# Half-row score matmuls, earlier gate chunks and later low parts in a two-block transformer kernel

## The chip, the cores and the metric

The kernel runs on one core of one Trainium2 chip. The metric is the device time of one execution in microseconds (us), the median of several. Five engines work side by side, each through its own list of instructions in a fixed order: TensorE (PE in the profile, with its weight loads as PEld), VectorE (DVE), ScalarE (ACT), GpSimd (POOL) and SyncE (SP), which only issues DMAs. They wait for each other by semaphores alone.

## The reference, cut to what matters

A token block of 256 rows and 1024 features passes through two layers of a first block and one layer of a second block. All data are float32.

```python
for l in range(2):                                   # first block
    xn = rms_norm(h, norm_g[l])
    a_q, a_k, a_v, i_q, i_k, i_w, ..., c_q, c_k, c_v, ... = split(xn @ w_in[l])
    # dsa: indexer scores of 4 heads, top-64 keys per query, then 8 heads of 64 features, one shared key
    score = einsum('bqh,bqhk->bqk', wi, relu(einsum('bqhd,bkd->bqhk', qi, ki)))
    # diff: 8 heads of 64 features, softmaxes mixed in pairs: p[0] - lam * p[1]
    # (three more branches: mla, sgu, memory)
    h = h + merged_branches @ w_out[l]
x = rms_norm(h, final_norm_g)
# second block
shift_a, scale_a, gate_a, shift_m, scale_m, gate_m = split(silu(c) @ w_ada + b_ada)   # 12 chunks of 512
h = rmsnorm(x, g_mix) * (1 + scale_a) + shift_a
gq, gk, gv, gr, gg, mq, mk, mv = split(h @ w_in)     # gla: 4 heads; moba: 8 heads of 64 features
o_moba = softmax(mq @ mk.T * 64**-0.5 + rel_bias, causal) @ mv
x = x + gate_a * (concat([o_gla, o_moba]) @ w_out)
h = rmsnorm(x, g_mlp) * (1 + scale_m) + shift_m
x = x + gate_m * (relu(h @ w_ff1) ** 2 @ w_ff2)
out = rmsnorm(x, g_final)
```

## The kernel before

**Tiling.** The 256 tokens are two tiles t=0, 1 of 128 rows; features are halves c=0, 1 of 512. Every large product is a sum of three matmuls in the fast float32 form: each operand is split into a high and a low part (`hi`, `lo` of the tokens; `wh` by ACT in L408 and `wl` by DVE in L409 for the weights), and wh·hi, wl·hi, wh·lo are added in PSUM (L470, L471, L473, and L493, L495, L496 for transposed results). A weight piece is 4 x 128 rows by up to 512 columns (1 MB), loaded by SP in the order of a list `pieces`; the loads run ahead as far as buffers are free. A result bank is evacuated by ACT or DVE.

**Order.** While one piece is multiplied, `half(k)` after each of its halves steps three lanes of side work (attention, small norms, the modulation) by one `yield`, and `defer(f, n)` runs f after n halves. A scheduler then orders the instructions of each engine by priority; `pin` keeps chosen instructions in program order, `behind(mark)` holds instructions behind a marked one, `tc.high_priority` pulls a chain ahead. Within an engine the resulting order is fixed.

**Scores.** A head has 64 features, and two heads lie above each other in a tile of 128 partitions. The kernel before multiplies on all 128 rows: `padded` writes the queries of a head into its own 64 rows of a zeroed tile (`qz`, `dz`), so that the other head's keys meet zeros (L973, L1005, L1051, L1474; plain float32, two passes for each matmul); for tile t=1 of dsa, `stacked` puts the high part of the query above its low part, and two fast matmuls (L678, L679) make a score. `attention` runs units of 2 or 4 heads through three stages: `s1` (scores into one PSUM bank, then `soft`: L718 row maximum on DVE, L721 exponent on ACT), `s2` (transposes L748, evacuated by ACT in L751 and DVE in L752) and `s3` (L768, probabilities times values).

**Modulation.** The vector silu(c) @ w_ada is made chunk by chunk by `ada(q, gate)`: two raw pieces of 1 MB, one DVE multiply (L1403) and seven multiply-adds (L1405) over 128x512, a split (L1414, L1415), and two matmuls against ones (L1419, L1420). Chunks 0 to 3 run in layer 0 and 6 to 9 in layer 1 of the first block (table `ADA`); 4 and 5 (`gate_a`) run in the second block while its `w_in` is multiplied, and 10, 11 later.

**Handovers.** At the end of the first block each half row of the residual gets its final norm and the second block's first norm at once (`row_norms`: L1247 adds the branch result, ACT's L694 sums squares, L1328 multiplies by the gain in place, L694 sums again; L1350, L1352 and a reciprocal root by DVE's L247 to L253 follow). `modulated` scales the row (L1358 on DVE and L1359 on ACT) and `to_operand_mod` transposes it on PE (L612), writes the high part on ACT (L654) and the low part by L659, L661 and L662. The same happens after the second block's `w_out` (`residual`, L1703 and L1704). Here PE needs the operand before it can go on.

Of the kernel before, what the change touches and what calls it, by code (L numbers as in the profile page):

```python
# [27 lines left out]
LOOK, AHEAD, WK, SLOTS = 3, 6, 7, 13  # L28
# [6 lines left out]
ADA = [(0, 1, 2, 3), (6, 7, 8, 9)]  # L35
# [22 lines left out]
def block_kernel(ctx: ExitStack, tc: tile.TileContext, a, out):  # L58
# [30 lines left out]
    def work(shape, tag="wk", dt=F32, bufs=None):  # L89
        n = 1  # L90
        for s in shape[1:]:
            n *= s
        own = tag in ("gains0", "gains1", "mb0", "mb1", "q0", "gg")
# [55 lines left out]
    marks = {}  # L149
# [225 lines left out]
    def run_stream():  # L375
# [20 lines left out]
        def split(i, by_k=False):  # L396
# [250 lines left out]
    def to_operand_mod(src, t, xo, am, bm, k0):  # L647

        tmp = work([128, 4, 128])
# [3 lines left out]
        for i, (sc, bi) in enumerate(cols):  # L653
            A.activation(hi[:, i, :], ps[i // 2][:, i % 2, :], AF.Identity, scale=sc, bias=bi)  # L654
        for b in range(0, 4, 2):
            for i in range(b, b + 2):
                sc, bi = cols[i]
                if b == 0 or k0 == 0:
                    V.tensor_scalar(tmp[:, i, :], ps[b // 2][:, i - b, :], sc, bi, op0=OP.mult, op1=OP.add)  # L659
                else:  # L660
                    A.activation(tmp[:, i, :], ps[1][:, i - 2, :], AF.Identity, scale=sc, bias=bi)  # L661
            ins = V.tensor_tensor(lo[:, b:b + 2, :], tmp[:, b:b + 2, :], hi[:, b:b + 2, :].bitcast(F32), OP.subtract)  # L662
        if k0 == 0:
            marks["lo", t] = ins

    def stacked(dst, ps):


        n = ps.shape[1]
        for b in range(2):  # L670
            own, other = (slice(64 * c, 64 * c + 64) for c in (b, 1 - b))
            to = slice(n * b, n * b + n)
            A.activation(dst[own, to, :], ps[own], AF.Copy)
            V.tensor_tensor(dst[other, to, :], ps[own], dst[own, to, :].bitcast(F32), OP.subtract)

    def stacked_mm(ps, q, hi, lo):

        T.matmul(ps, q, hi, start=True, stop=False)  # L678
        T.matmul(ps, q, lo, start=False, stop=True)  # L679

    def padded(dst, ps, scale=1.0):


        n = ps.shape[1]
        for b in range(2):
            own = slice(64 * b, 64 * b + 64)
            A.activation(dst[own, n * b:n * b + n, :], ps[own], AF.Copy, scale=scale)
# [9 lines left out]
    def attention(units, finish, nheads, dv, d=1):  # L697
# [8 lines left out]
        def soft(u, heads):  # L706

            nh, nk = len(heads), u["nk"]
            ps = bbank([128, nh, nk])
            for k, h in enumerate(heads):  # L710
                u["score"](ps[:, k, :], h, u["t"], nk)
# [20 lines left out]
        def s1(i):  # L732
            u = units[i]
            p, rs = soft(u, u["heads"])
            if u.get("combine"):
                p2, rs2 = soft(u, u["heads2"])
# [105 lines left out]
    def layer(l, h):  # L842
# [81 lines left out]
        def dsa_prep():  # L924
# [11 lines left out]
            q0 = work([128, 2, 128], "q0", bufs=1)  # L936

            q1, i1, ks = (slot(d).bitcast(F32R) for d in ([128, 8, 128], [128, 4, 128], [128, 4, 256]))
            yield
            for t in range(2):  # L940
                ps = transpose4(aq[:, t, :])
                if t:
                    stacked(q1, ps)
                else:
                    padded(dz[:, 0:8, :], ps)
                ps = bbank([128, 4, 128])
                for i, src in enumerate((kd[:, t, 0:128], kd[:, t, 128:256], a2[:, t, 128:256],
                                         a2[:, t, 256:384])):
# [14 lines left out]
            for t in range(2):  # L963
                nk = 128 * (t + 1)
                acc = work([128, nk], "acc")
                R = {}
                for b in range(2):
                    ps = bbank([128, 2, nk])
                    for p in range(2):
                        if t:  # L970
                            stacked_mm(ps[:, p, :], i1[:, 2 * b + p, :], ks[:, 1, :], ks[:, 3, :])
                        else:
                            T.matmul(ps[:, p, :], dz[:, 8 + 2 * b + p, :], q0[:, 1, :], start=True, stop=True)  # L973
                    R[b] = work([128, 2, nk], "P")
                    A.activation(R[b], ps, AF.Relu)
# [16 lines left out]
            L["dsa"] = (q0, q1, ks, mb)  # L992
            lanes[0].add(dsa_attn())

        def dsa_attn():
            q0, q1, ks, mb = L["dsa"]
# [3 lines left out]
            def score(ps, hh, t, nk):  # L1000
                i = 4 * (hh % 2) + hh // 2
                if t:
                    stacked_mm(ps, q1[:, i, :], ks[:, 0, :], ks[:, 2, :])
                else:
                    T.matmul(ps, dz[:, i, :], q0[:, 0, :], start=True, stop=True)  # L1005
            units = [dict(t=t, heads=hs, outs=hs, nk=128 * (t + 1), score=score, scale=64 ** -0.5,
                          bias=lambda k, t=t: mb[t], v=lambda hh, b: a2[:, b, 64:128])
# [11 lines left out]
        def diff_prep():  # L1019
# [16 lines left out]
            kT = slot([128, 4, 256])  # L1036
            for t in range(2):
                padded(qz[:, :, tsl(t)], transpose4(cq[:, t, :]))
# [3 lines left out]
            L["diff"] = (kT, nl, dg)  # L1042
            lanes[0].add(diff_attn())

        def diff_attn():
            kT, nl, dg = L["diff"]
# [3 lines left out]
            def score(ps, hh, t, nk):  # L1050
                T.matmul(ps, qz[:, 4 * (hh % 2) + hh // 2, tsl(t)], kT[:, hh // 2, 0:nk], start=True, stop=True)  # L1051
# [272 lines left out]
    def row_norms(t, c):  # L1324
# [3 lines left out]
        V.tensor_tensor(hc, hc, B["fg"][:, c * 512:(c + 1) * 512], OP.mult)  # L1328
# [4 lines left out]
        v = mean_so_far(("y", t), hc, c, 0.0)  # L1333
        if c == 0:
            return
        def back():
# [4 lines left out]
        for c in range(2):  # L1341
            defer(lambda c=c: rest(c), 3 - t)
# [13 lines left out]
    def modulated(t, r, xo, am, bm):  # L1356
# [35 lines left out]
    def ada(q, gate=None):  # L1392

        st = {}
        for j in range(2):
# [13 lines left out]
            def fin():  # L1409
# [11 lines left out]
                if gate is None:  # L1421
# [45 lines left out]
    def moba_attn():  # L1467
        for _ in range(2):
            yield
        kT = B["mT"]  # L1470
        o = slot([128, 2, 512])

        def score(ps, hh, t, nk):
            T.matmul(ps, qz[:, 4 * (hh % 2) + hh // 2, tsl(t)], kT[:, hh // 2, 0:nk], start=True, stop=True)  # L1474
        units = []
        for p in range(2):
            for q in range(2):
# [425 lines left out]
```

## Time and profile before

| | us |
|---|---|
| median of 3 runs (lowest, highest) | 1221.54 (1221.0, 1221.8) |
| the profiled execution | 1220.62 |
| its span, first to last instruction | 1218.9 |
| PE busy | 1201.0 (99%) |
| DVE busy | 904.1 (74%) |
| ACT busy | 672.5 (55%) |
| POOL busy | 34.0 (3%) |

The profile is of one execution. Times are from the span's start. "Busy" is the union of an engine's instructions; matmuls overlap, so the records of one group can sum to more than they cost. Between 30 and 890 us the two layers of the first block run, from 890 to 905 the handover to the second block, from 905 its `w_in`, moba and gla, from 1008 its `w_out`, from 1023 to 1042 the second handover, then the feed-forward part.

### The profile page before, as it was taken

Reading aid. Unit: us, or ns where it says so; the run is one execution under the profiler, and the core shown is the slowest. Engines: PE = TensorE matmul, PEld = TensorE weight load, DVE = VectorE, ACT = ScalarE, POOL = GpSimd, SP = SyncE. Lnnn points to the kernel's source line nnn. Section 1 sums busy time; section 2 is a strip of 40 time slices with the busy share of each in tenths; the row PEclk is TensorE's granted clock in tenths of the full one; section 3 lists DMA queues with packets and bytes.
Section 4 is the critical chain, followed back from the end, with each engine's and each line's share of the span. In section 5 each row is a group of like instructions: output and inputs, shape, how many; then the busy total and the mean of one; then the engine's idle time right before and its main releaser. Section 6 shows DMA issues by size and latency. Waiting matters only on the chain.

```text
span 1218.9 us, 17443 instructions
## 1 busy us (share of the span) xinstructions
PE 1201.0 (99%) x6589; PEld 1039.3 (85%) x6589; DVE 904.1 (74%) x1889; ACT 672.5 (55%) x1188; POOL 34.0 (3%) x68
## 2 busy tenths in 40 slices
PE   9999999999999999999999999999999899999997
PEld 7888988898888888898888988888879787898996
DVE  5996777659886776776877688776788778766755
ACT  5765455547566455546544766654465556545442
POOL 4000000000000000000000000000020010000000
PEclk9999999999999999999999999999999999999999
DMA  9866646454566466655566445655547634666740
GB/s 310 305 230 212 202 141 216 134 175 157 179 210 205 138 219 196 233 174 173 164 221 194 149 151 171 227 190 182 166 138 265 207 114 137 233 218 221 255 145 35
DMA packets 117828, 231.31 MB, mean 190 GB/s; under 512 B 4604, under 2 KB 14496, under 8 KB 117616
## 3 DMA queue, kind: packets, MB, share of 16 engines
q1 hardware_dynamic: 114640, 221.62, 54.6%
q0 software_dynamic: 2640, 7.78, 2.1%
q8 instruction: 52, 0.85, 0.3%
q10 hardware_dynamic: 464, 0.79, 0.2%
q14 instruction: 32, 0.26, 0.1%
HBM read 229.10 MB, written 2.63 MB: 190 GB/s over the span
## 4 chain that ended last, share of the span: by engine, by line
PE 92%; DVE 3%; ACT 2%; DMA 1%; issue 1%; ACTq 0%
PE pm L471 22%; PE pm L470 22%; PE pm L473 22%; PE pm L493 4%; PE pm L495 4%; PE pm L496 4%; PE po L768 3%; PE pm L612 3%; PE pm L748 2%; DMA wt<-in_w_in_dram 1%; PE pm L1164 1%; PE pm L1051 1%; DVE wl L409 1%; ACT j L694 1%; ACT hi L654 1%
## 5 line engine op out<-in xcount | busy, mean ns | idle before, releaser
L409 DVE TENSOR_TENSOR wl<-wt,wh 128x1024 fp32r<-128x1024 f32 (+6 forms) x388 | 443.3, 1170 | 163.6 <-ACT wh L408 162.6
L408 ACT ACTIVATE wh<-wt 128x1024 fp32r<-128x1024 f32 (+6 forms) x388 | 379.6, 1014 | 254.4 <-PE pm L473 141.7
L470 PE MATMUL pm<-wh,hi 128*128 128x512 f32 (+4 forms) x1288 | 500.1, 390 | 0.0
L471 PE MATMUL pm<-wl,hi 128*128 128x512 f32 (+4 forms) x1288 | 490.2, 382 | 0.8 <-DVE wl L409 0.8
L473 PE MATMUL pm<-wh,lo 128*128 128x512 f32 (+4 forms) x1288 | 337.2, 382 | 0.5 <-DVE lo L662 0.5
L471 PEld LDWEIGHTS pm<-wl,hi 128*128 128x128 f32 x1288 | 242.3, 188 | 44.9 <-DVE wl L409 2.1
L470 PEld LDWEIGHTS pm<-wh,hi 128*128 128x128 f32 x1288 | 242.1, 188 | 43.3 <-issue 0.3
L473 PEld LDWEIGHTS pm<-wh,lo 128*128 128x128 f32 x1288 | 237.5, 188 | 47.4 <-DVE lo L662 2.2
L493 PE MATMUL pm<-hi,wh 128*128 128x256 f32 x416 | 118.9, 286 | 0.0
L496 PE MATMUL pm<-hi,wl 128*128 128x256 f32 x416 | 117.7, 283 | 0.0
L495 PE MATMUL pm<-lo,wh 128*128 128x256 f32 x416 | 117.7, 283 | 0.0
L493 PEld LDWEIGHTS pm<-hi,wh 128*128 128x128 f32 x416 | 79.7, 192 | 1.4 <-issue 1.0
L495 PEld LDWEIGHTS pm<-lo,wh 128*128 128x128 f32 x416 | 79.8, 192 | 0.4
L496 PEld LDWEIGHTS pm<-hi,wl 128*128 128x128 f32 x416 | 79.7, 192 | 0.0
L721 ACT ACTIVATE w<-w,s 128x256 f32<-128x256 f32 (+1 forms) x112 | 49.8, 446 | 35.6 <-DVE s L718 35.6
L1405 DVE SCALAR_TENSOR_TENSOR w<-wt,cact,w 128x512 f32<-128x512 f32 x84 | 62.7, 747 | 1.6 <-DMA wt<-in_w_ada_dram 0.6
L768 PEld LDWEIGHTS po<-t,w 128*128 128x128 f32 x352 | 45.9, 191 | 7.0 <-ACT w L751 3.4
L1210 ACT ACTIVATE t<-pm,s 128x512 f32<-128x512 f32 x40 | 27.5, 689 | 40.7 <-PE pm L473 40.6
L768 PE MATMUL po<-t,w 128*128 128x64 f32 (+1 forms) x352 | 45.2, 270 | 3.3 <-ACT w L751 3.0
L612 PE MATMUL pm<-ident,t 128*128 128x128 f32 (+1 forms) x316 | 42.3, 273 | 2.1 <-DVE t L1358 2.0
L612 PEld LDWEIGHTS pm<-ident,t 128*128 128x128 f32 (+1 forms) x316 | 36.8, 138 | 8.5 <-issue 2.2
L694 ACT ACTIVATE j<-t 128x512 f32<-128x512 f32 (+3 forms) x59 | 28.1, 477 | 28.0 <-DVE t L1794 15.7
(318 smaller groups left out, 1043.7 us busy)
## 6 DMA issues: line engine op xcount, KB each, us to landing
wt<-in_w_in_dram SPq DMA_DIRECT2D x96, 1024.0 KB, 5.1
wt<-in_w_ff_dram SPq DMA_DIRECT2D x32, 1024.0 KB, 5.8
wt<-in_w_ada_dram SPq DMA_DIRECT2D x24, 1024.0 KB, 5.2
wt<-in_w_branch_dram SPq DMA_DIRECT2D x20, 1024.0 KB, 5.2
wt<-in_w_out_dram SPq DMA_DIRECT2D x12, 1024.0 KB, 5.2
wt<-in_mem_w_kv_dram SPq DMA_DIRECT2D x8, 1024.0 KB, 5.2
wt<-in_w_in_dram SPq DMA_DIRECT2D x4, 904.0 KB, 4.8
wt<-in_w_in_dram SPq DMA_DIRECT2D x4, 768.0 KB, 4.4
```

What stands on the lines that cost most here:

```text
L408: pin(A.activation(hv[:, ks], wv[:, ks], AF.Copy), on)
L409: pin(V.tensor_tensor(lv[:, ks], wv[:, ks], hv[:, ks].bitcast(F32), OP.subtract), on)
L470: pin(T.matmul(ps[:, :n], xh, hi[:, i, :n], start=first and i == 0, stop=False), on)
L471: pin(T.matmul(ps[:, :n], xh, lo[:, i, :n], start=False, stop=False), on)
L473: ins = pin(T.matmul(ps[:, :n], xo.lo[:, k0 + i, tsl(t)], hi[:, i, :n], start=False, stop=last and i == nk - 1), on)
L493: T.matmul(ps, wh, xh, start=first and i == 0 and c % 2 == 0, stop=False, skip_group_check=True)
L495: T.matmul(ps, wh, xl, start=False, stop=False, skip_group_check=True)
L496: T.matmul(ps, wl, xh, start=False, stop=last and i == nk - 1, skip_group_check=True)
L612: T.transpose(ps[:, i, :], src[:, i * w:(i + 1) * w], ident)
L721: A.activation(p[:, k, :], p[:, k, :], AF.Exp, bias=mx[:, k:k + 1], scale=-1.0, accum_out=sm[:, k:k + 1])
L768: T.matmul(opsum[t][:, h, :], pt[:, k * nb + b, :], u["v"](h, b), start=b == 0, stop=b == nb - 1)
L1405: V.scalar_tensor_tensor(acc, w[:, i, :], B["c"][:, k:k + 1], acc, op0=OP.mult, op1=OP.add)
```

## The change

**Scores.** `stacked`, `stacked_mm`, `padded` and the tiles `qz`, `dz`, `q0` go, with six memsets on POOL at the start. Queries are copied whole (`qT`), and `score64` multiplies a head's 64 query rows by its 64 key rows in plain float32: even heads on rows 0 to 63, odd heads on rows 64 to 127. `scores` opens two PSUM banks, one for the even and one for the odd heads, and issues their matmuls in turn, pinned in program order. Units with `pair` share such a call: the second unit's bank is filled together with the first one's.

**Gate chunks.** Chunks 4 and 5 move into the tables of layers 0 and 1. Their result is kept as one row, added to its bias row, written to a DRAM tile `garow` by POOL, and broadcast to 128 partitions by a POOL DMA when the second block's `w_out` begins (`output_begins`).

**Low parts.** `to_operand_mod` writes the high parts at once and returns a function that makes the low ones; after `w_out`, that function for tile 0 is held behind the multiply of the residual (`behind("mul")`). `row_norms` writes the product with the gain to a tile of its own instead of in place. Weight splits that were held behind the low parts of tile 1 are held behind its high parts too. `SLOTS` grows from 13 to 16 tiles; the row sums of the first x half are deferred by three halves instead of one.

```diff
-LOOK, AHEAD, WK, SLOTS = 3, 6, 7, 13
+LOOK, AHEAD, WK, SLOTS = 3, 6, 7, 16
-ADA = [(0, 1, 2, 3), (6, 7, 8, 9)]
+ADA = [(0, 1, 2, 3, 4), (6, 7, 8, 9, 5)]
...
-            with behind(("lo", 1), id(pieces[i]) in after_norm):
+            held = id(pieces[i]) in after_norm
+            with behind(("lo", 1), held), behind(("hi", 1), held):
...
-                defer(lambda t=t: row_stats(t, c, 0), 1)
+                defer(lambda t=t: row_stats(t, c, 0), 1 if c else 3)
...
         for i, (sc, bi) in enumerate(cols):
-            A.activation(hi[:, i, :], ps[i // 2][:, i % 2, :], AF.Identity, scale=sc, bias=bi)
-        for b in range(0, 4, 2):
...
+            ins = A.activation(hi[:, i, :], ps[i // 2][:, i % 2, :], AF.Identity, scale=sc, bias=bi)
         if k0 == 0:
-            marks["lo", t] = ins
...
+            marks["hi", t] = ins
+
+        def low():
+            tmp = work([128, 4, 128])
+            for b in range(0, 4, 2):
...
+                lo_ins = V.tensor_tensor(lo[:, b:b + 2, :], tmp[:, b:b + 2, :], hi[:, b:b + 2, :].bitcast(F32),
+                                         OP.subtract)
...
+        return low
+
+    def rows_of(h):
+
+        return slice(64 * (h % 2), 64 * (h % 2) + 64)
+
+    def score64(ps, qT, kT, h, t, nk, kp=None):
+
+        hb = rows_of(h)
+        pin(T.matmul(ps, qT[hb, h // 2, tsl(t)], kT[hb, h // 2 if kp is None else kp, 0:nk], start=True, stop=True))
...
+        def scores(u, *heads):
+
+            banks = [bbank([128, len(hs), u["nk"]]) for hs in heads]
+            for k in range(len(heads[0])):
+                for ps, hs in zip(banks, heads):
+                    u["score"](ps[:, k, :], hs[k], u["t"], u["nk"])
+            return banks
...
-            p, rs = soft(u, u["heads"])
+            if u.get("pair"):
+                if i % 2 == 0:
+                    u["ps"], units[i + 1]["ps"] = scores(u, u["heads"], units[i + 1]["heads"])
+                banks = [u.pop("ps")]
+            elif u.get("combine"):
+                banks = scores(u, u["heads"], u["heads2"])
...
             def score(ps, hh, t, nk):
-                T.matmul(ps, qz[:, 4 * (hh % 2) + hh // 2, tsl(t)], kT[:, hh // 2, 0:nk], start=True, stop=True)
+                score64(ps, qT, kT, hh, t, nk)
...
-        V.tensor_tensor(hc, hc, B["fg"][:, c * 512:(c + 1) * 512], OP.mult)
+        if c == 0:
+            B["h", t] = slot([128, D])
+        yc = B["h", t][:, c * 512:(c + 1) * 512]
+        V.tensor_tensor(yc, hc, B["fg"][:, c * 512:(c + 1) * 512], OP.mult)
...
-                if gate is None:
+                if q in (4, 5):
+                    row = work([1, 512])
+                    G.dma_start(row, a["b_ada_2"][0:1, q * 512:(q + 1) * 512])
+                    V.tensor_tensor(row, ps[0:1, :], row, OP.add)
+                    if "garow" not in B:
+                        B["garow"] = drm.tile([1, D], F32, name="garow")
+                    G.dma_start(B["garow"][:, csl(q - 4)], row)
...
-        for p in range(2):
-            for q in range(2):
+        for q in range(2):
+            for p in range(2):
...
-        spread(first + 4, [lambda: ada(4, ("ga", 0)), lambda: ada(5, ("ga", 1))])
...
+                    low = []
+
                     def second():
+                        with behind("mul", t == 0):
+                            low[0]()
                         with behind("res", t == 0):
-                            rest(1)
-                    defer(lambda: rest(0), 2)
+                            rest(1)()
+                    defer(lambda: low.append(rest(0)), 2)
                     defer(second, 3 - t)
...
+        def output_begins():
+            run_until("moba")
+            B["ga"] = slot([128, D])
+            d = B["garow"]
+            G.dma_start(B["ga"], bass.AP(tensor=d.tensor, offset=d.offset, ap=[[0, 128], [1, D]]))
```

Line numbers shift: the splits L408 and L409 become L401 and L402, the products L470, L471 and L473 become L464, L465 and L467, the transposes L612 and L748 become L606 and L749, L768 becomes L769, L654 becomes L648, L659 and L662 become L658 and L661, L1247 and L1328 become L1229 and L1313, L1703 and L1704 become L1699 and L1700.

Three places in the engines' lists follow, of the kernel before and of the changed one. On PE in moba, before: the scores of a unit are two matmuls of 128 rows (L1474) into one bank, between the transposes of the unit before, and the products with the values (L768) follow.

```order
L748 MATMUL pm_9041<-ident,w_8986 128x128 [waits Activation_49]
L748 MATMUL pm_9041<-ident,w_8986 128x128
L1474 MATMUL pm_9049<-t_8884,qz 128x256
L748 MATMUL pm_9041<-ident,w_8986 128x128 [waits Activation_49]
L748 MATMUL pm_9041<-ident,w_8986 128x128
L1474 MATMUL pm_9049<-t_8884,qz 128x256
L473 MATMUL pm_8954<-wh_8937,lo_8247 128x512 x2
L768 MATMUL po_9074<-t_9039,w_9046 128x64 [waits Activation_49] x2
L768 MATMUL po_9074<-t_9039,w_9046 128x64 [waits DVE_49]
L768 MATMUL po_9074<-t_9039,w_9046 128x64
L748 MATMUL pm_9082<-ident,w_9055 128x128 [waits Activation_49]
L748 MATMUL pm_9082<-ident,w_9055 128x128
```

On PE at the same place of the changed kernel: the four matmuls L675 of two units go into two banks in turn, and three products with the values (L769) stand within them.

```order
L769 MATMUL po_9020<-t_8988,w_8995 128x64 [waits Activation_49]
L749 MATMUL pm_9028<-ident,w_9001 128x128 [waits Activation_49]
L749 MATMUL pm_9028<-ident,w_9001 128x128
L749 MATMUL pm_9028<-ident,w_9001 128x128 [waits Activation_49]
L749 MATMUL pm_9028<-ident,w_9001 128x128
L675 MATMUL pm_9036<-t_8850,t_8717 128x256 [waits PE_49]
L769 MATMUL po_9020<-t_8988,w_8995 128x64 [waits Activation_49]
L769 MATMUL po_9020<-t_8988,w_8995 128x64 [waits DVE_49]
L769 MATMUL po_9020<-t_8988,w_8995 128x64
L675 MATMUL pm_9037<-t_8850,t_8717 128x256
L675 MATMUL pm_9036<-t_8850,t_8717 128x256
L675 MATMUL pm_9037<-t_8850,t_8717 128x256
```

What moved: the scores of a unit no longer stand alone before it but two units' together, and one of three such groups in moba is parted by L769.

On DVE at the first handover, before: tile 0's residual sum (L1247), then L1352, which waits for ACT's sum of squares, then the gain (L1328).

```order
L1247 TENSOR_TENSOR t_87<-t_87,pm_8145 128x512 [waits PE_49]
L1352 TENSOR_SCALAR s_8255<-s_8254 128x1 [waits Activation_49]
L1328 TENSOR_TENSOR t_87<-t_87,t_8093 128x512 [waits DMASW7_49,DVE_49]
L1247 TENSOR_TENSOR t_87<-t_87,pm_8197 128x512 [waits PE_49]
L1352 TENSOR_SCALAR s_8261<-s_8260 128x1 [waits Activation_49]
L1350 SCALAR_TENSOR_TENSOR s_8281<-s_8280,s_8255 128x1 [waits Activation_49]
L1328 TENSOR_TENSOR t_87<-t_87,t_8093 128x512 [waits DVE_49]
```

In the changed kernel the product with the gain (L1313) goes to a tile of its own.

```order
L1229 TENSOR_TENSOR t_87<-t_87,pm_8121 128x512 [waits PE_49]
L1313 TENSOR_TENSOR t_8243<-t_87,t_8077 128x512 [waits DMASW2_49,DVE_49]
L1338 TENSOR_SCALAR s_8239<-s_8238 128x1 [waits Activation_49]
L1229 TENSOR_TENSOR t_87<-t_87,pm_8177 128x512 [waits PE_49]
L1338 TENSOR_SCALAR s_8246<-s_8245 128x1 [waits Activation_49]
L1313 TENSOR_TENSOR t_8243<-t_87,t_8077 128x512 [waits DVE_49]
L1336 SCALAR_TENSOR_TENSOR s_8266<-s_8265,s_8239 128x1 [waits Activation_49]
```

What moved: the gain stands ahead of the wait for ACT, and ACT's second sum of squares follows from it.

On DVE at the second handover, before: after the first half's residual (L1703, L1704) the low parts of tile 0 (L659, L662), then the residual of the second half.

```order
L1703 TENSOR_TENSOR w_9695<-pm_9538,t_8851 128x512 [waits PE_49]
L1704 TENSOR_TENSOR t_88<-t_88,w_9695 128x512 [waits DVE_49]
L659 TENSOR_SCALAR w_9703<-pm_9704,s_9631,adaT 128x128 [waits Activation_49]
L659 TENSOR_SCALAR w_9703<-pm_9704,s_9631,adaT 128x128
L659 TENSOR_SCALAR w_9703<-pm_9707,s_9631,adaT 128x128 [waits Activation_49]
L662 TENSOR_TENSOR lo_9625<-w_9703,hi_9624 128x2x128 [waits DVE_49]
L659 TENSOR_SCALAR w_9703<-pm_9707,s_9631,adaT 128x128
L1352 TENSOR_SCALAR s_9699<-s_9698 128x1 [waits Activation_49]
L1703 TENSOR_TENSOR w_9732<-pm_9572,t_8851 128x512 [waits PE_49]
```

In the changed kernel the second half's multiply (L1699) stands ahead of them.

```order
L1699 TENSOR_TENSOR w_9638<-pm_9481,t_9478 128x512 [waits PE_49]
L1700 TENSOR_TENSOR t_8308<-t_8308,w_9638 128x512 [waits DVE_49]
L1699 TENSOR_TENSOR w_9668<-pm_9515,t_9478 128x512 [waits PE_49]
L658 TENSOR_SCALAR w_9688<-pm_9646,s_9574,adaT 128x128 [waits Activation_49]
L658 TENSOR_SCALAR w_9688<-pm_9646,s_9574,adaT 128x128
L658 TENSOR_SCALAR w_9688<-pm_9649,s_9574,adaT 128x128 [waits Activation_49]
L661 TENSOR_TENSOR lo_9568<-w_9688,hi_9567 128x2x128 [waits DVE_49]
L658 TENSOR_SCALAR w_9688<-pm_9649,s_9574,adaT 128x128
```

What moved: the low parts of tile 0 come after the multiply of tile 1's second half, which waits for PE. Further down that list, L1780 (the final gain's scaling, 128x1024, L1774 before) now stands directly behind the last low part L661 of tile 1 and ahead of the next split L402 and of L1837 (L1831 before, the square of the feed-forward part).

## Rows read from the trace of the kernel before

**Rows 1.** The page: busy time by engine, and the chain that ended last.

```profile
PE 1201.0 (99%) x6589; PEld 1039.3 (85%) x6589; DVE 904.1 (74%) x1889; ACT 672.5 (55%) x1188; POOL 34.0 (3%) x68
PE 92%; DVE 3%; ACT 2%; DMA 1%; issue 1%; ACTq 0%
```

**Rows 2.** Stretches of the span: length, busy us (instructions) by engine, PEclk, DMA share, GB/s.

```profile
30.00:890.00 860.00, 860.00 (x4547) 742.65 (x4546) 654.60 (x1415) 484.20 (x863) 10.16 (x18) 1.00 0.58 189
905.00:950.00 45.00, 45.00 (x319) 42.03 (x319) 39.11 (x71) 24.43 (x38) 0.81 (x3) 1.00 0.68 233
950.00:955.50 5.50, 5.50 (x28) 4.54 (x27) 5.50 (x12) 4.52 (x10) 0.00 (x0) 1.00 0.88 279
955.50:959.00 3.50, 0.53 (x3) 0.12 (x2) 3.36 (x4) 3.50 (x7) 0.00 (x0) 1.00 0.59 176
959.00:965.00 6.00, 5.26 (x24) 4.23 (x25) 4.60 (x20) 3.26 (x9) 0.00 (x0) 0.72 0.89 305
```

**Rows 3.** What PE waited for: engine, line, total us, times, longest.

```profile
PE po L768 <- ACT w L751: 3.0, 1, 3.0
PE pm L612 <- DVE t L1358: 2.0, 3, 1.1
PE pm L471 <- DVE wl L409: 0.8, 1, 0.8
```

**Rows 4.** PE groups by form: total us, mean ns | idle us.

```profile
L1051 PE MATMUL pm<-t,qz 128*128 128x256 f32 x32 | 7.6, 379 | 0.0
L1051 PE MATMUL pm<-t,qz 128*128 128x128 f32 x32 | 3.9, 275 | 0.0
L678 PE MATMUL pm<-t,t 128*128 128x256 f32 x24 | 6.6, 302 | 0.0
L1474 PE MATMUL pm<-t,qz 128*128 128x256 f32 x16 | 5.4, 443 | 0.0
```

**Rows 5.** PE timeline at a dsa burst: start us, us, instruction.

```profile
161.01 0.28 PE L678 MATMUL pm<-t,t 128*128 128x256 f32 x1
161.13 0.28 PE L679 MATMUL pm<-t,t 128*128 128x256 f32 x1
```

**Rows 6.** PE timeline around a burst of 64-row matmuls (gla).

```profile
975.06 0.61 PE L1474 MATMUL pm<-t,qz 128*128 128x128 f32 x4
975.60 0.72 PE L1583 MATMUL pm<-t,w 64*128 64x128 f32 x8
976.25 0.50 PE L470 MATMUL pm<-wh,hi 128*128 128x512 f32 x1
976.59 0.40 PE L471 MATMUL pm<-wl,hi 128*128 128x512 f32 x1
```

**Rows 7.** The same burst, begun by 975.81 and by 975.92.

```profile
975.60 0.39 PE L1583 MATMUL pm<-t,w 64*128 64x128 f32 x2
975.60 0.50 PE L1583 MATMUL pm<-t,w 64*128 64x128 f32 x4
```

**Rows 8.** ACT timeline ahead of PE's longest wait.

```profile
955.03 3.04 ACT L408 ACTIVATE wh<-wt 128x1024 fp32r<-128x1024 f32 x4 [0.25 <-DMA wt<-in_w_in_dram]
958.46 0.37 ACT L751 ACTIVATE w<-pm 128x256 f32<-128x256 f32 x1
```

**Rows 9.** The page: groups of the modulation's multiply-adds.

```profile
L1405 DVE SCALAR_TENSOR_TENSOR w<-wt,cact,w 128x512 f32<-128x512 f32 x84 | 62.7, 747 | 1.6 <-DMA wt<-in_w_ada_dram 0.6
```

**Rows 10.** PE, DVE and ACT timelines of the first handover.

```profile
898.40 0.16 DVE L1350 SCALAR_TENSOR_TENSOR s<-s,s 128x1 f32<-128x1 f32 x1 [0.25 <-ACT j L694]
898.61 0.66 ACT L408 ACTIVATE wh<-wt 128x544 fp32r<-128x544 f32 x1
902.37 1.06 PE L612 MATMUL pm<-ident,t 128*128 128x128 f32 x8 [1.09 <-DVE t L1358]
```

**Rows 11.** DVE and PE timelines of the second handover and behind it.

```profile
1027.65 0.68 DVE L1703 TENSOR_TENSOR w<-pm,t 128x512 f32<-128x512 f32 x1
1049.40 0.68 DVE L1774 TENSOR_SCALAR t<-t 128x1024 f32<-128x1024 f32 x1
```

More of the change, by code (lines that the diff above doesn't have):

```diff
@@ L663, in to_operand_mod @@
-        if k0 == 0:
-            marks["lo", t] = ins
[L666 to L679, printed above, removed]
@@ L704, in attention, with soft @@
             left[u["t"]] = left.get(u["t"], 0) + 1
[L706 to L711, printed above, removed]
+        def scores(u, *heads):
[4 more added lines that the diff above has]
+            return banks
+        def soft(u, ps):
+            nh, nk = ps.shape[1], ps.shape[2]
             mx, rs, sm = small(nh), small(nh), small(nh)
@@ L966, in dsa_prep @@
                 R = {}
+                banks = [bbank([128, 2, nk]) for _ in range(2)]
+                for hh in range(4):
+                    score64(banks[hh % 2][:, hh // 2, :], ik, ik, hh, t, nk, 3)
                 for b in range(2):
-                    ps = bbank([128, 2, nk])
-                    for p in range(2):
[L970 to L973, printed above, removed]
                     R[b] = work([128, 2, nk], "P")
-                    A.activation(R[b], ps, AF.Relu)
+                    A.activation(R[b], banks[b], AF.Relu)
                 prev = cmf[:, 256 - nk:]
@@ L991, in dsa_prep @@
                 yield
-            L["dsa"] = (q0, q1, ks, mb)
+            L["dsa"] = (qT, ik, mb)
             lanes[0].add(dsa_attn())
         def dsa_attn():
-            q0, q1, ks, mb = L["dsa"]
+            qT, ik, mb = L["dsa"]
             a2 = L["a2"]
@@ L1000, in score @@
             def score(ps, hh, t, nk):
[L1001 to L1005, printed above, removed]
+                score64(ps, qT, ik, hh, t, nk, 2)
             units = [dict(t=t, heads=hs, outs=hs, nk=128 * (t + 1), score=score, scale=64 ** -0.5,
-                          bias=lambda k, t=t: mb[t], v=lambda hh, b: a2[:, b, 64:128])
+                          pair=True, bias=lambda k, t=t: mb[t], v=lambda hh, b: a2[:, b, 64:128])
                      for t, hss in ((1, ((0, 2), (1, 3), (4, 6), (5, 7))), (0, ((0, 2, 4, 6), (1, 3, 5, 7))))
@@ L1469, in moba_attn @@
             yield
-        kT = B["mT"]
+        qT, kT = B["qT"], B["mT"]
         o = slot([128, 2, 512])
         def score(ps, hh, t, nk):
-            T.matmul(ps, qz[:, 4 * (hh % 2) + hh // 2, tsl(t)], kT[:, hh // 2, 0:nk], start=True, stop=True)
+            score64(ps, qT, kT, hh, t, nk)
         units = []
-        for p in range(2):
-            for q in range(2):
+        for q in range(2):
+            for p in range(2):
                 hs = (4 * q + p, 4 * q + p + 2)
@@ L1483, in moba_attn @@
         for u in units:
-            u.update(outs=u["heads"], nk=128 * (u["t"] + 1), score=score, scale=1.0,
+            u.update(pair=True, outs=u["heads"], nk=128 * (u["t"] + 1), score=score, scale=1.0,
                      v=lambda hh, b: B["mv"][:, b, hh * 64:(hh + 1) * 64])
@@ L1672, in eq @@
         def eq(b, ps):
-            for z in range(2):
-                own = slice(64 * z, 64 * z + 64)
-                A.activation(qz[own, 4 * z + 2 * b:4 * z + 2 * b + 2, :], ps[own], AF.Copy, scale=64 ** -0.5)
+            if b == 0:
+                B["qT"] = slot([128, 4, 256])
+            A.activation(B["qT"][:, 2 * b:2 * b + 2, :], ps, AF.Copy, scale=64 ** -0.5)
         def ek(b, ps):
```

83 lines of the change are left out of this document (35 added, 48 removed).

## The prediction

> **What bounds the kernel now.** I read the page first, the engines' busy times and the chain that ended last [rows 1]: PE is busy for 1201.0 of 1218.9 us and makes 92% of the chain. So only two things shorten the time: fewer or shorter instructions on PE, and PE's own gaps. The stretches say where the gaps are [rows 2]. From 30 to 890 us, in both layers of the first block, PE is busy for 860.00 of 860.00 us, while DVE has 654.60; work taken off DVE, ACT or the DMAs is worth nothing there, and work added there costs nothing as long as PE keeps its cover. The largest hole lies in moba: from 955.5 to 959 PE works 0.53 of 3.50 us, and from 959 to 965 it has 0.74 us of idle time and a mean granted clock of 0.72. At the two levels of 1.2 and 2.4 GHz that mean is 6.00 x 0.28 = 1.68 us of lost full-clock time, and the fall came right behind the idle stretch. Third, the waits of PE by releaser [rows 3]: 3.0 us in one piece for ACT's L751 (this hole), three waits of 2.0 us together for the scaled rows of L1358 (the two handovers), 0.8 us for a weight split at the start.
>
> **Scores, on PE.** Forms and counts [rows 4] and starts give the price. A float32 pass of 128 columns takes 0.112 us: four of L1474 span 0.61, less the 0.275 of one, over three [rows 4, 6]; one of 256 columns I take as twice that, 0.22. The fast matmuls L678 and L679 start 0.12 apart [rows 5]. Before there are 48 of these (24 each), 48 passes of 256 columns (32 in L1051, 16 in L1474) and 96 of 128 (32 in L1051; 32, 16 and 16 in L1005, L973 and L1474): 5.8 + 10.6 + 10.8 = 27.1 us.
>
> After, all 96 score matmuls are two passes each on 64 rows. No score of before runs on half the rows, but gla's L1583 does, eight passes, four on each half [rows 6]: they span 0.72 us, that is last start 0.45 behind the first. One after the other at 0.112 it would be 0.78. The windows show why: two have begun by 975.81 and four by 975.92 [rows 7], so they run in pairs, one on each half. But the burst isn't cheap. L1474's last pass ends its 0.112 at 975.51, the next full-row matmul starts at 976.25, and the one behind it 0.34 later where 0.23 is usual: 0.85 us in all, against 0.45 of streaming. The other 0.41 is paid for entering and leaving.
>
> So: 48 heads x 2 passes x 0.22 / 2 + 48 x 2 x 0.112 / 2 = 10.6 + 5.4 = 16.0 us of streaming. Bursts: two of the indexer, three of dsa and three of diff per layer, three in moba, and one more since L769 parts a group there: 20 x 0.41 = 8.2. 24.2 in place of 27.1: -2.9 us. It is not uniform: for t=1 of dsa and the indexer the burst of four heads rises from 8 x 0.12 = 0.96 to 1.3, and the gain is that of t=0, diff and moba.
>
> On this the Trainium skill has two rules on one page, "TensorEngine Tiling (Array Packing)". By its section Theoretical Speedup, 64 rows bring up to 2x; by that alone this term would be -11 us. Its Key Properties say that a change of tiling mode drains TensorE, which speaks against short bursts; the 0.41 us of the gla burst agrees with it [rows 6].
>
> If the two banks of a burst aren't free together, PE waits at its head. A bank of a pair is now held while the first half of the pair goes through softmax. Price by bounds: zero, as no score waits now and PE is full [rows 2], to 0.4 us a burst in the layers, 16 bursts, 6.4 us, with the 0.4 a softmax step's own size (0.37 of L751 as the nearest row [rows 8]). I take zero, since all of a burst's steps lie between pieces of main products.
>
> **Gate chunks.** Two chunks of 8 DVE instructions of about 0.75 us each [rows 9] are 12 us; with their splits and adds some 13 us of DVE leave the stretch of 905 to 959, where DVE has 39.11 of 45 us busy and then all of it [rows 2]. They go to the layers, 6.5 us to each of two stretches of some 430 us, of which DVE uses three quarters: hidden. The 4 MB of weights too: the DMAs are at 0.58 there. In moba the DMAs are at 0.68 and then 0.88 with them, and PE's 3.0 us wait is preceded on ACT by a split L408 that itself waited for its DMA, 3.04 us of splits ahead of the L751 that PE needs, which starts at 958.46 [rows 8]. Late weights, then a backlog on ACT, then PE: both ends shrink when 4 MB fewer are loaded and DVE has 13 us less. Besides, PE's new list has main products between most attention steps there. The hole is 2.97 + 0.74 + 1.68 = 5.4 us. I take -5.0; bounds -6.0 (what the bank of pairs brings beyond) and 0. Chunk 4 and 5's bias rows and `garow` queue on POOL before gla's gate DMAs and memsets; POOL is busy 0.81 of 45 us there [rows 2], so nothing there is late.
>
> **First handover.** DVE's L1350 waited for ACT's sum of squares at 898.40, and ACT put a split of 0.66 us ahead of the next sum at 898.61 [rows 10]. PE's largest wait there is 1.09 us [rows 10]. With the gain in a tile of its own L1313 no longer waits for the first sum, and the splits stand behind the high parts: two splits (1.3 us) and one wait (0.25) leave the chain, 1.5 us, more than PE waits. But the splits held back are needed by the next product soon after: I take -1.3 of the 1.6 us lost there (1.09 and half a us in smaller waits), bounds -2.0 and +0.5.
>
> **Second handover.** The splits leave ACT's chain here too, but the DVE list puts L1699 of the second half ahead of tile 0's low parts. Before, that multiply started at 1027.65, when its bank was complete [rows 11]; the low parts were written before it. PE needs them in the next product and then waits for one multiply (0.68) and three 128-column steps, less what is left of its queue: +0.5. L1780, 0.68 us [rows 11], now stands ahead of L1837, on which the feed-forward transposes wait: +0.6 at most. Against these stand the splits: about -0.5. Together +0.6; bounds -1.0 and +1.5.
>
> **Start.** The row sums of the first x half leave ACT's way to the second piece, whose split made PE wait for 0.8 us [rows 3]. I take -0.4, since later pieces are bound by their DMAs; bounds -0.9 and 0.
>
> **Sum.** 1220.6 - 2.9 - 5.0 - 1.3 - 0.4 + 0.6 = 1211.6 for a profiled execution; the median of before is 0.9 above its profiled one, so 1212.5.
>
> **The rivals.** *The moba wait stays.* For it: DVE was full before and ACT too, and a pair puts two softmaxes of work behind one burst, so ACT's L751 can be late without the chunks. Against: the late weights came with the chunks. If 3 to 5 us stay: 1215.5 to 1217.5.
>
> *The pairs wait for their banks*, up to 6.4 us: 1219. It needs all 16 bursts to wait; the full PE of the layers [rows 2] speaks for spare time of DVE and ACT there.
>
> *The halves don't overlap in these bursts, slower.* The order here is even, odd, even, odd with 128x256 results into two banks; gla's was two and two. If each pass streams alone, it is 31.9 + 8.2 = 40.1 us for 27.1: +13.0, so 1212.5 + 15.9 = 1228.4. From the sum, of the 15.9 us of overlap 9 must be lost before the kernel is slower. Against it: the pairs of rows 7.
>
> **How the numbers follow.** A change of 0.2%, 2.4 us, is what can be told from none. The forecast has 0.58: 1209.5 to 1215. The moba wait staying has 0.18. Better than 1209.5, both handovers and the start at their best ends, 0.08. Banks 0.10, of which about two thirds lie within 0.2% of before. No overlap 0.06, slower. So faster 0.85, same 0.08, slower 0.07. The range, 1208.5 to 1219, holds all but the slower case and the ends of the others.
>
> **What would show it.** In the stretch of moba PE's wait for ACT's evacuation (L751's successor) is gone and PEclk stays at 1.00: right; a wait of over 2 us there: the first rival. The 64-row matmuls L675 start two at a time, a burst of four heads with 128x256 taking about 1.3 us net: right; evenly spaced starts: the last rival. Idle time of PE directly ahead of L675: banks. PE's waits for the scaled rows at the first handover fall below 0.5 us, and a wait for low parts appears at the second. If PE waits anywhere between 30 and 890 us for DVE or ACT, the cover that I assumed for the moved chunks failed, and the prediction with it.

## The result and the profile after

| | before | changed |
|---|---|---|
| median, us (lowest, highest) | 1221.55 (1221.0, 1221.8) | 1229.2 (1226.37, 1231.29) |
| ratio, 95% interval | | 1.0062 (1.004 to 1.0084) |
| profiled execution, us | 1220.62 | 1230.17 |

The changed kernel is slower, where 1212.5 was forecast. Its four executions were granted a mean clock of 0.991 (1230.17 and 1231.29 us) or 0.995 (1226.37 and 1228.22); the profiled one has 0.991. Its page has PE busy for longer and the same engine in the chain, against [rows 1]:

```profile
PE 1206.1 (98%) x6589; PEld 1035.2 (84%) x6589; DVE 898.3 (73%) x1875; ACT 664.7 (54%) x1170; POOL 33.2 (3%) x65
PE 91%; DVE 4%; DMA 2%; ACT 2%; issue 1%; ACTq 0%; SPq 0%; DVEq 0%
```

The waits of PE say where to look. Columns as in [rows 3].

```profile
PE pm L464 <- ACT hi L620: 3.0, 2, 2.1
PE po L769 <- ACT w L752: 2.8, 2, 2.5
PE po L769 <- DVE w L753: 1.3, 2, 0.9
...
PE pm L606 <- DVE w L1837: 1.1, 1, 1.1
PE pm L467 <- DVE lo L661: 1.1, 3, 0.6
PE pm L606 <- DVE t L1344: 1.0, 3, 0.5
```

The first three are not handovers and not moba. They lie between 30 and 890 us, where PE never waited before [rows 2]. The stretches, columns as in [rows 2]:

```profile
30.00:460.00 430.00, 427.10 (x2290) 366.40 (x2290) 325.27 (x708) 238.83 (x421) 7.01 (x13) 0.99 0.60 197
460.00:890.00 430.00, 425.50 (x2186) 361.22 (x2185) 323.86 (x689) 232.10 (x417) 6.20 (x10) 0.99 0.58 189
...
207.00:210.40 3.40, 1.29 (x8) 0.86 (x6) 0.84 (x1) 2.98 (x5) 0.53 (x1) 1.00 0.49 179
210.40:217.20 6.80, 6.01 (x24) 4.42 (x25) 4.07 (x17) 2.04 (x8) 0.00 (x0) 0.50 0.48 157
...
585.00:589.20 4.20, 2.11 (x13) 1.66 (x12) 3.85 (x6) 3.20 (x7) 0.53 (x1) 1.00 0.14 18
589.20:593.00 3.80, 3.80 (x11) 2.97 (x11) 2.77 (x8) 0.00 (x0) 0.00 (x0) 0.55 0.74 259
...
817.00:821.40 4.40, 2.90 (x17) 2.12 (x16) 3.38 (x7) 2.98 (x8) 0.52 (x1) 1.00 0.16 21
821.40:828.20 6.80, 6.80 (x35) 6.80 (x34) 2.98 (x18) 2.45 (x13) 0.56 (x1) 0.50 0.65 220
...
955.00:965.00 10.00, 10.00 (x63) 8.39 (x62) 5.68 (x8) 5.50 (x9) 0.00 (x0) 1.00 0.28 75
```

By the first two, PE is idle for 2.9 and 4.5 us in the layers. Three times it idles for 1.5 to 2.1 us in a few us and is then granted the lower clock, for 6.8, 3.4 and 6.8 us: half of these 17 us, 8.5, is lost too. Together 15.5 us, since 0.8 us of the idle time lies within the first of these stretches. The last row is the place of moba's hole: PE is full at the full clock, as forecast.

The whole loss shows when the same product is looked up in both traces. Main products are the matmuls of the six product lines (L470, L471, L473, L493, L495 and L496 before), counted by their starts. The 64th and the 3542nd of them, before:

```profile
30.14 0.39 PE L471 MATMUL pm<-wl,hi 128*128 128x512 f32 x1
891.12 0.39 PE L471 MATMUL pm<-wl,hi 128*128 128x512 f32 x1
```

and in the changed kernel:

```profile
31.19 0.39 PE L465 MATMUL pm<-wl,hi 128*128 128x512 f32 x1
907.97 0.39 PE L465 MATMUL pm<-wl,hi 128*128 128x512 f32 x1
```

From one to the other it takes 876.78 us for 860.98: 15.8 more, where 1.9 less was forecast (the layers' part of the scores' 2.9). So 17.7 us are lost in the layers; e1's expectation has 17.6, from the spacing of the starts.

What PE did around the first of the three, as its timeline:

```profile
206.31 1.08 PE L467 MATMUL pm<-wh,lo 128*128 128x512 f32 x4
207.22 0.39 PE L1409 MATMUL pm<-w,onesr 128*128 128x512 f32 x1
207.46 0.39 PE L1410 MATMUL pm<-w,onesr 128*128 128x512 f32 x1
207.69 0.60 PE L749 MATMUL pm<-ident,w 128*128 128x128 f32 x4
210.79 1.12 PE L769 MATMUL po<-t,w 128*128 128x64 f32 x4 [2.50 <-ACT w L752]
...
214.39 2.08 PE L675 MATMUL pm<-t,t 64*128 64x256 f32 x8
216.40 1.47 PE L606 MATMUL pm<-ident,t 128*128 128x128 f32 x8
217.71 1.00 PE L769 MATMUL po<-t,w 128*128 128x64 f32 x8
218.60 0.50 PE L464 MATMUL pm<-wh,hi 128*128 128x512 f32 x1
```

No main product stands between 207.2 and 218.6. An attention step follows directly on the one that feeds it, with the evacuation of L749's bank by ACT in between, and ACT has other work first:

```profile
207.42 0.69 ACT L1192 ACTIVATE t<-pm,s 128x512 f32<-128x512 f32 x1 [1.39 <-PE pm L467]
208.01 0.57 ACT L1420 ACTIVATE w<-pm 1x512 f32<-1x512 f32 x1
208.49 1.99 ACT L401 ACTIVATE wh<-wt 128x1024 fp32r<-128x1024 f32 x2
210.38 0.36 ACT L752 ACTIVATE w<-pm 128x256 f32<-128x256 f32 x1
```

The code says why steps follow on each other. Each stream piece of `w_branch` calls `run_until(("og", n, l))`, which steps all lanes at once until the branch's gated operand exists. That operand is made by `og()` in lane 2, one turn for every two halves. The tail of a modulation chunk, `fin()`, sits in the same lane and takes six turns. Before, with four chunks in a layer, `run_until` never had to step in a layer. With five it steps eleven times, at five branches. The same eleven steps come in e3 and e9 below; in e1, e2, e4 and e10 there are none.

### The profile page after: what moved, and what is told of

Read it like the earlier page. It is cut to its first block, busy times and chain, and to the rows that moved or that the text cites. A ratio compares the mean times of both kernels' runs of the same rounds, so it can differ in the third digit from the quotient of the medians.

```text
span 1228.5 us, 17398 instructions
## 1 busy us (share of the span) xinstructions
PE 1206.1 (98%) x6589; PEld 1035.2 (84%) x6589; DVE 898.3 (73%) x1875; ACT 664.7 (54%) x1170; POOL 33.2 (3%) x65
## 4 chain that ended last, share of the span: by engine, by line
PE 91%; DVE 4%; DMA 2%; ACT 2%; issue 1%; ACTq 0%; SPq 0%; DVEq 0%
PE pm L464 22%; PE pm L467 22%; PE pm L465 22%; PE pm L487 4%; PE pm L490 4%; PE pm L489 4%; PE po L769 3%; PE pm L606 3%; DMA wt<-in_w_in_dram 2%; PE pm L675 2%; PE pm L749 2%; DVE wl L402 1%; PE pm L1146 1%; ACT wh L401 1%; PE pm L916 1%
## 5 line engine op out<-in xcount | busy, mean ns | idle before, releaser
L402 DVE TENSOR_TENSOR wl<-wt,wh 128x1024 fp32r<-128x1024 f32 (+6 forms) x388 | 443.9, 1171 | 185.3 <-ACT wh L401 185.0
L401 ACT ACTIVATE wh<-wt 128x1024 fp32r<-128x1024 f32 (+6 forms) x388 | 379.4, 1016 | 272.1 <-PE pm L467 151.0
L464 PE MATMUL pm<-wh,hi 128*128 128x512 f32 (+4 forms) x1288 | 500.8, 390 | 3.0 <-ACT hi L620 3.0
L465 PE MATMUL pm<-wl,hi 128*128 128x512 f32 (+4 forms) x1288 | 490.7, 382 | 0.8 <-DVE wl L402 0.8
L467 PE MATMUL pm<-wh,lo 128*128 128x512 f32 (+4 forms) x1288 | 337.8, 382 | 1.3 <-DVE lo L661 1.1
L464 PEld LDWEIGHTS pm<-wh,hi 128*128 128x128 f32 x1288 | 242.4, 188 | 50.1 <-ACT hi L620 3.5
L465 PEld LDWEIGHTS pm<-wl,hi 128*128 128x128 f32 x1288 | 242.5, 188 | 44.4 <-DVE wl L402 1.4
L467 PEld LDWEIGHTS pm<-wh,lo 128*128 128x128 f32 x1288 | 238.0, 188 | 49.0 <-DVE lo L661 3.4
L769 PEld LDWEIGHTS po<-t,w 128*128 128x128 f32 x352 | 47.4, 197 | 8.1 <-ACT w L752 3.5
L769 PE MATMUL po<-t,w 128*128 128x64 f32 (+1 forms) x352 | 47.5, 277 | 4.1 <-ACT w L752 2.8
L606 PE MATMUL pm<-ident,t 128*128 128x128 f32 (+1 forms) x316 | 42.8, 276 | 1.0 <-DVE t L1344 1.0
L606 PEld LDWEIGHTS pm<-ident,t 128*128 128x128 f32 (+1 forms) x316 | 37.0, 140 | 7.5 <-issue 1.9
```

The costliest lines, as they stand in the source:

```text
L401: pin(A.activation(hv[:, ks], wv[:, ks], AF.Copy), on)
L402: pin(V.tensor_tensor(lv[:, ks], wv[:, ks], hv[:, ks].bitcast(F32), OP.subtract), on)
L464: pin(T.matmul(ps[:, :n], xh, hi[:, i, :n], start=first and i == 0, stop=False), on)
L465: pin(T.matmul(ps[:, :n], xh, lo[:, i, :n], start=False, stop=False), on)
L467: ins = pin(T.matmul(ps[:, :n], xo.lo[:, k0 + i, tsl(t)], hi[:, i, :n], start=False, stop=last and i == nk - 1), on)
L606: T.transpose(ps[:, i, :], src[:, i * w:(i + 1) * w], ident)
```

## The experiments

Theory A: the two tails' turns in the shared lane delay the operands; the stream then drains the lanes without cover, PE waits, and its clock falls. Theory B: the chunks' own DVE, DMA and PE work doesn't fit in the layers. Theory C: two banks for each score burst make PE wait.

| | median us | ratio to before, 95% interval |
|---|---|---|
| e1, tails in a lane of their own | 1212.72 | 0.9926 (0.9913 to 0.9939) |
| e2, gate chunks back | 1220.67 | 0.9995 (0.9987 to 1.0004) |
| e3, gate chunks alone | 1231.29 | 1.0086 (1.0071 to 1.0101) |
| e4, scores alone | 1220.36 | 0.9995 (0.9986 to 1.0003) |
| e5, e1 with memsets at the start | 1211.72 | 0.9924 (0.9911 to 0.9938) |
| e6, e1 with the second handover's order back | 1211.65 | 0.9923 (0.9911 to 0.9936) |
| e7, e1 with e5 and e6 | 1210.22 | 0.9909 (0.9894 to 0.9924) |
| e8, e1 with scores bank by bank | 1215.0 | 0.9951 (0.9938 to 0.9963) |
| e9, before with empty turns | 1238.63 | 1.0141 (1.0127 to 1.0154) |
| e10, before with the lane alone | 1221.28 | 1.0 (0.9991 to 1.0008) |

**e1, the tails in a lane of their own.**

```diff
-    lanes = [Lane(), Lane(), Lane()]
+    lanes = [Lane(), Lane(), Lane(), Lane()]
...
             lanes[2].step()
+            lanes[3].step()
...
-                    lanes[2].add(fin())
+                    lanes[3].add(fin())
```

> The changed kernel, with the tails of the modulation chunks (split, two matmuls, row) in a lane of their own instead of the lane that also makes the branches' gated operands. All work and both gate chunks stay in the first block. Theory A (the two more chunks delay the operands in that shared lane, so the stream has to drain the lanes without main products, PE waits there and its clock falls): PE's gaps between 30 and 890 us, 17.6 us beyond the score bursts' own cost, go; 1211 to 1213 us. Theory B (the chunks' own DVE, DMA and PE work is what the layers can't hide): as the changed kernel, 1226 to 1231. Theory C (two banks for each score burst make PE wait): also 1226 to 1231.

1212.72 us: A, and neither B nor C, as all the work and all the bursts are still there. The layers' stretches of e1:

```profile
30.00:460.00 430.00, 429.94 (x2322) 369.33 (x2321) 330.02 (x714) 242.59 (x426) 7.03 (x13) 1.00 0.61 201
460.00:885.00 425.00, 424.90 (x2210) 361.03 (x2209) 323.66 (x694) 232.00 (x418) 8.00 (x13) 1.00 0.58 190
```

PE is full there again at the full clock, with the chunks' DVE work beside it. From the 64th to the 3542nd main product e1 takes 0.94 us less than before, and e2, without the two chunks, 2.00 less. So the chunks cost the layers 1.06 us, about what their own four matmuls on PE take (L1409 and L1410 in the changed kernel, 0.24 us from one start to the next).

**e9, empty turns, nothing else.** To see the turns without the work, the kernel before gets a fifth chunk in each layer that does nothing.

```diff
+        if q is None:
+            def empty():
+                for _ in range(6):
+                    yield
+            piece(wsrc(a["w_ada_2"][0], 0, 4, 0, 8), 4, 8, lambda w: None, raw=True)
+            piece(wsrc(a["w_ada_2"][0], 0, 4, 0, 8), 4, 8, lambda w: lanes[2].add(empty()), raw=True)
+            return
```

> The kernel before with one empty chunk more in each layer of the first block: two loads of 16 KB in the stream that nothing reads, and a generator of six empty turns in the shared lane, where the changed kernel has the tail of chunk 4 or 5. Gate chunks 4 and 5 stay in the second block with all their work. Theory A (turns of the lane are what costs): PE waits in the layers at the same five places as with the gates alone, which lost 5.6 us of busy time more at a lower clock in places, and moba's hole stays: 1229 to 1238. If the chunks' work was what cost: 1221, as before.

1238.63 us, 17.5 over before and 0.6 above A's range: six empty turns a layer cost as much as the layers lost in the changed kernel (between the same two main products 16.4 us more than before, for 15.8 there). PE's waits in e9 (L470, L751 and L768 are before's lines):

```profile
PE po L768 <- ACT w L751: 6.0, 3, 3.7
PE pm L470 <- ACT hi L626: 4.3, 2, 3.4
```

The first holds moba's 3.7, which stays, beside two new ones; the second is new.

**e10, the lane alone.** e1's edit on the kernel before.

> The kernel before with the lane of its own alone, chunks 4 and 5 in the second block. Theory A: no drain of the lanes happens before, so there is nothing to win: 1221, within 1 us. If the lane speeds up the branches in itself: below 1219.

No change (1221.28 us), as A has it: without a drain the lane is worth nothing.

**e3 and e2, the gate chunks alone and the rest without them.** e3 is the kernel before with this and the `garow` lines of the change:

```diff
-ADA = [(0, 1, 2, 3), (6, 7, 8, 9)]
+ADA = [(0, 1, 2, 3, 4), (6, 7, 8, 9, 5)]
```

> The kernel before with the gate chunks alone moved into the first block. A and B: the layers wait as in the changed kernel (10 to 18 us) and moba's hole of 5.4 us goes: 1226 to 1234. C: no new wait, 1216.

1231.29 us, so the loss needs no score burst. e2 is the reverse edit on the changed kernel.

> The changed kernel with gate chunks 4 and 5 back in the second block, scores, low parts and all else as changed. A and B: PE full again from 30 to 890 us, and some of moba's wait for late weights is back: 1214 to 1218. C: the layers still wait, 1226 or more.

1220.67 us, above the range of A and B and below that of C. C falls, since PE has 430.00 of 430.00 and 425.00 of 425.00 us in the layers. But moba's hole is back and dearer than I had it:

```profile
PE po L769 <- ACT w L752: 3.4, 1, 3.4
PE pm L1409 <- ACT w L1404: 1.9, 1, 1.9
```

The second wait is for a chunk's split in moba, which before had none, and the lower clock was granted twice, for 3.4 and 6.8 us. Against e1 the chunks in the first block, without drains, save 8.0 us; but from the 3713th to the 4012th main product, the stretch of moba and gla, e2 takes 3.0 us longer than the kernel before, and why it does wasn't tested.

**e4, the scores alone.** The kernel before with `score64`, `scores`, `pair` and no zeroed tiles.

> The kernel before with the scores alone changed (64 rows, even and odd heads in turn, two banks, no zeroed tiles, no memsets at the start). A and B: bursts of 0.85, 1.27 and 1.29 us in place of the old ones, 2.9 us less, about 1 us given back at the start where GpSimd's loads now come earlier: 1218.5 to 1220.5. C: waits in the layers, 1225 or more.

1220.36 us, within the expectation, though an interval of 0.9986 to 1.0003 doesn't tell it from no change. Its PE is full in both layers too. The trace tells more: from the 64th to the 3542nd main product e4 takes 1.99 us less than before, as the sum has it for the layers (1.9), and the 64th starts 1.1 us later.

**e8, does the turn-taking matter?**

```diff
-            for k in range(len(heads[0])):
-                for ps, hs in zip(banks, heads):
+            for ps, hs in zip(banks, heads):
+                for k in range(len(heads[0])):
...
-                for hh in range(4):
+                for hh in (0, 2, 1, 3):
```

> The kernel with the lane of its own, with the scores of a burst issued bank by bank: all even heads, then all odd ones, in place of in turn. If TensorE overlaps the two halves only with neighbours in its list: some of 15.9 us lost, up to 1228. If it reaches past the neighbour, as in gla's bursts of two and two: 1212.7, within 1 us.

1215.0 us, 2.3 more than e1: between the two. Bursts of four heads keep their time, bursts of eight don't. PE's timeline in e8, one of each:

```profile
203.97 1.14 PE L676 MATMUL pm<-t,t 64*128 64x256 f32 x8
...
233.21 1.71 PE L676 MATMUL pm<-t,t 64*128 64x128 f32 x16
```

and the second of them in e1:

```profile
233.12 1.16 PE L676 MATMUL pm<-t,t 64*128 64x128 f32 x16
```

0.55 us for each of four bursts in the layers and one in moba: 2.7, against 2.3 measured.

**e6, the second handover.** On e1:

```diff
-                        with behind("mul", t == 0):
-                            low[0]()
...
-                    defer(lambda: low.append(rest(0)), 2)
+                    defer(lambda: rest(0)(), 2)
...
+                    if f == 1 and c == 0:
                         V.tensor_scalar(B["gf"], B["gf"], SCALED, None, op0=OP.mult)
```

> The kernel with the lane of its own, with the low parts at the second handover made at once again, and the final gain scaled one piece of the feed-forward part later. If the residual's multiply ahead of the low parts and the 0.68 us of the final gain are what PE waits for at the second handover (1.1 us for low parts, 1.1 for the feed-forward square): 1.0 to 1.6 us less, 1211.1 to 1211.7. Rival, the splits are what is late: same, 1212.7.

1211.65 us, 1.1 less than e1. The two intervals overlap, but the traces bear it out: from the 4012th to the 4199th main product, across this handover, e6 takes 1.1 us less than e1. PE's waits for low parts are half a us, 1.3 in e1; the 1.1 for the square stays:

```profile
PE pm L607 <- DVE w L1835: 1.1, 1, 1.1
...
PE pm L468 <- DVE lo L662: 0.5, 2, 0.3
```

So the low parts' order paid. The other edit didn't reach DVE: in e6's list the scaling of the final gain (L1778) still stands directly behind the last low part and ahead of the square (L1835), and what its place costs stays untested.

```profile
1027.12 0.76 DVE L662 TENSOR_TENSOR lo<-w,hi 128x256 fp32r<-128x256 f32 x2
1027.80 0.69 DVE L1778 TENSOR_SCALAR t<-t 128x1024 f32<-128x1024 f32 x1
1028.40 2.35 DVE L403 TENSOR_TENSOR wl<-wt,wh 128x1024 fp32r<-128x1024 f32 x2
1030.67 0.69 DVE L1835 SCALAR_TENSOR_TENSOR w<-pm,w 128x512 f32<-128x512 f32 x1
```

**e5 and e7, the start.** On e1 and on e6:

```diff
+    fill = cst.tile([128, 256], F32, name="fill")
+    for _ in range(11):
+        G.memset(fill, 0.0)
```

> The kernel with the lane of its own, and 11 memsets of 128x256 on GpSimd at the start in the place of the zeroed tiles' ones, so that GpSimd's loads are issued some 3.3 us later, as before. If these loads slow the first x tile (PE waits 0.8 us there, 0.5 before): 0.5 to 1.2 us less than 1212.7. If the start is bound by its own loads: 1212.7.

> The lane of its own, the low parts at once at the second handover, the later final gain, and the memsets at the start. If the two gains of about 1.0 us over the lane alone add: 1210.4 to 1211.0. If that of the memsets was the spread of the runs (its profile shows the wait for the first x tile longer, not shorter): 1211.6.

The medians are 1.0 and 1.4 us lower than e1's and e6's (e7's lies 0.2 below its range for gains that add), yet the profile shows no gain at the start. Nor did the edit do what was meant: one memset came between every two of GpSimd's loads, and the first load (`posi`) was issued 2.9 us earlier than before, not as before. First the kernel before, then e5:

```profile
5.57 0.66 POOL L182 DMA_DIRECT2D posi<-in_positions_dram  x1
```

```profile
2.39 0.31 POOL L207 MEMSET fill<- 128x256 f32 x1
2.64 0.66 POOL L182 DMA_DIRECT2D posi<-in_positions_dram  x1
3.29 0.34 POOL L207 MEMSET fill<- 128x256 f32 x1
```

PE's wait for the first x in e5:

```profile
PE pm L634 <- DMA t<-in_x_dram: 1.5, 1, 1.5
```

It is 1.2 in e3, which has the old memsets, and 0.8 in e1, which has none. The first score burst starts at 122.9 us in e5 and at 123.0 in e1. The lower clock was granted for 3.4 us in each, at 7.8 us in e5, behind that wait, and at 928.6 in e1, so from the profiles the lower median can't be put down to the start, whose term stays open. e7 has the lowest median: 1210.22 us, 0.9909 of before, with an interval that overlaps those of e5 and e6.

## Why the prediction was wrong

The step that failed is the gate chunks' "They go to the layers ...: hidden". The work was hidden but for 1.06 us of PE time, as e1 and e2 show. What I didn't price was its place in a lane: I counted instructions, loads and queues, but not the turns that its generator takes from the one behind it. In place of 0 they cost the layers some 17 us: 17.7 lost in the changed kernel, 16.7 of them gone in e1, and empty turns alone cost 17.5 in e9. The condition at the end of the prediction, PE waiting between 30 and 890 us, is what happened; its cause isn't a lack of DVE time. The rival for the slower side, halves that don't overlap, was the wrong one.

The forecast by stretch, against the profiled executions (us more than before, from main product to main product; e10, which has nothing to win, shows the spread):

| up to the main product | forecast | changed | e1 | e10 |
|---|---|---|---|---|
| 64th, start | -0.4 | +1.05 | +0.74 | +0.79 |
| 3542nd, layers | -1.9 | +15.80 | -0.94 | -0.01 |
| 3713th, first handover | -1.3 | -0.39 | -0.71 | +0.05 |
| 4012th, moba and gla | -6.0 | -7.57 | -5.63 | +0.14 |
| 4199th, second handover | +0.6 | +0.67 | +0.67 | -0.02 |

The scores' 2.9 stand as 1.9 in the layers and 1.0 in moba. e1's -5.63 holds the lower clock at 928.6 us; e5 and e6 have -8.13 there.

The other steps, by the changed kernel's profile:

- *Scores, -2.9.* Right, as e4's layers show (-1.99). A burst of four heads in the layers, with the matmuls next to it:

```profile
203.30 1.13 PE L675 MATMUL pm<-t,t 64*128 64x256 f32 x8
204.37 0.50 PE L464 MATMUL pm<-wh,hi 128*128 128x512 f32 x1
204.70 0.40 PE L465 MATMUL pm<-wl,hi 128*128 128x512 f32 x1
```

By starts it costs 1.27 us, 0.86 of streaming and 0.40 of change, where 1.3 was taken; bursts of eight heads at t=0 cost 1.29. All 20 cost 23.6 us at the full clock, 24.2 forecast. That the change of mode drains the array, as the Trainium skill has it ("TensorEngine Tiling (Array Packing)", Key Properties), agrees with the 0.40.
- *Moba's hole, -5.0.* Right: it is gone in the changed kernel and in e1. Of the changed kernel's 7.6 us, 1.0 is the scores' part and about 1.1 the chunks' own matmuls, which moved; 5.5 are left.
- *First handover, -1.3.* Too much. PE's waits there are 0.18, 0.27 and 0.54 us, for 1.09 [rows 10] and 0.27 before: -0.4. The "half a us in smaller waits" was this 0.27 alone. A new wait of 0.5 us for a small copy follows at 944.
- *Second handover, +0.6.* Right, 2.2 us of waits for 1.7 before. The waits for low parts grew by 0.6 us, by the row named: L1699 waits for PE and the low parts come after it. The wait for the square grew by 0.6 too, to 1.1; that the final gain ahead of it is the cause is argued and not shown.

```profile
1035.46 0.69 DVE L1699 TENSOR_TENSOR w<-pm,t 128x512 f32<-128x512 f32 x1 [1.25 <-PE pm L467]
1036.07 1.04 DVE L658 TENSOR_SCALAR w<-pm,s,adaT 128x128 f32<-128x128 f32 x3
```

- *Start, -0.4.* Not shown. The 64th main product starts at 30.14 us before and at 31.19 in the changed kernel, but in e9, e3 and e10, which issue the same memsets and loads up to there as the kernel before, at 29.32, 30.24 and 30.93: the change is no clear step out of this spread.

The sum 1212.5 is e1's 1212.72 within its spread, but partly by luck: moba gave more than forecast (8.1 us in e5 and e6, scores' part included, for 6.0), start and first handover less. With the layers' 17.7 the forecast for a profiled execution, 1211.6, becomes 1229.3, for 1230.17 measured.

## What to carry to other kernels

Where side work runs in queues by turns, price a moved task by the turns that it takes from what stands behind it, and look for the place where the program must wait for that. In the list of the engine that sets the pace, search the whole of it for steps that follow each other with no main work between; I looked at moba and the handovers, and the row at 207 us stood in the list as plainly. Here an idle time of about two us cost about as much again by the lower clock behind it (7.4 us of idle time in the layers, 8.5 us by the clock).

## What the runs showed that I had not expected

TensorE overlapped half-row matmuls of 64 rows also when two on one half stood ahead of two on the other (1.14 us for 1.13 in turn, e8 and the changed kernel), but not fully with four and four (1.71 for 1.16). The Trainium skill ("TensorE: Matmul & The Clock Gate", Part 3: Packing small matmuls) says matmuls start in the program's order, strictly; in gla's burst and in e8 two and two ran in pairs, so here the measurement decides.

The lower clock came behind idle stretches as short as 1.5 us among short dependent steps (817 to 821 us), but 0.9 us of idle time at 751 us was not followed by it.
